# One layer, its first weight columns and its first norm: the order on ScalarE and the queues of the constant rows

## The chip, the core and the metric

The kernel runs on one core of a Trainium2 chip. The core has a matrix engine (TensorE, PE in the profile; its weight loads are PEld), a vector engine (VectorE, DVE), an engine for functions and scaled copies (ScalarE, ACT), a general one (GpSimd, POOL) and one that here only issues transfers (SyncE, SP). ACT and POOL issue transfers too. The metric is the device time of one execution in microseconds, the median of several runs.

## The reference

A hybrid decoder layer on one sequence of 2048 rows of 1024 numbers, in 32-bit floats:

```python
h = _rmsnorm(x, norm1_w[l])
proj = h @ w_in[l]
hg_p, rw_p = proj[..., :HG_COLS], proj[..., HG_COLS:]
...
o_hg = _hgrn2_mixer(q_raw, f_raw, i_raw, g_raw, lower_bounds[l], hg_norm_w[l])
rw_p = rw_p + (_token_shift(rw_p) - rw_p) * rw_shift_mu[l]
...
o_rw = _rwkv7_mixer(r, k, v, wd, ad, gd, ...)
x = x + jnp.concatenate([o_hg, o_rw], axis=-1) @ w_out[l]
x = x + _conv_ffn(_rmsnorm(x, norm2_w[l]), w_up[l], conv_w[l], conv_b[l], w_down[l])
```

with `_rmsnorm(x, w) = x * rsqrt(mean(x * x) + 1e-6) * w`. For the change only the first two lines matter: the norm of x and the product with `w_in` (1024 x 3840, thirty columns of 128).

## The kernel before

**Blocks and columns.** The sequence is worked in four blocks of 512 rows. For each block, `w_in` is taken in columns of 128: a job ("P") computes one column for 512 rows as eight steps over the inner dimension (`KD = 8`, index k). Every 32-bit operand is split into a high part and the rest (names ending in h and l), and a step is three matmuls, `wh*hh`, `wh*hl` and `wl*hh` (`mm3`), so a column is 24 matmuls into one bank (`pj`), which is then evicted by ScalarE and VectorE (`ev`). The first column is evicted by `ev_lora` (a scaled copy, two additions on VectorE, then a Tanh).

**The weights.** `load(i)` fetches column i as two halves (`wraw`, four buffers) by POOL's queue, and `split` makes `wh` with a cast on ScalarE (`S.copy`, line 249) and `wl` with a subtraction on VectorE (line 250). In the first block both parts are also stored to memory (`Win...`, four stores of 256 KB a column, POOL's queue), from where the later blocks read them. `wh` and `wl` have four buffers each, two columns' worth.

**The beginning.** Four tiles of 128 rows of x go by SP's queue into `first`. The small vectors (norm weights, biases and so on: eleven inputs, then `hg_lb_logits`) are loaded as rows of one 128 x 128 tile, `rows` (lines 143 to 149), alternately by POOL's and by ScalarE's queue; TensorE transposes it (`vps`), and VectorE copies it to `vt`, whose columns are the vectors. The norm of the first block (lines 151 and 152) is for each tile a square with a sum on ScalarE (`nsq`), a logarithm and an exponential (`nst`), and a scaling of x on VectorE. Then `transposed` turns the normed x on TensorE in eight groups of four transpositions (k = 0 to 7, six banks at hand, `hg` and `rw`), and `to_h` makes `hh` of each with a scaled copy on ScalarE and `hl` on VectorE (line 481). Job 0 calls for two of these groups first, then for one ahead of each of its eight steps.

**What sets the order.** The program states data flow; a scheduler orders the instructions of each engine by priority (earlier in the program first) and by its own model of when an instruction can start. Each engine then runs its list strictly in order, so an instruction that waits holds all behind it on that engine, issues of transfers among them. `tc.add_manual_dep(a, b, NOSYNC)` puts a behind b in that order without a wait of its own. ScalarE's functions need tables: `act` loads the table set when the function asks for another one, and puts the load behind all uses of the set before (`tab["uses"]`). Scaled copies (`AF.Copy`) and squares need none and are not in that list.

Of the kernel before, what the change touches and what calls it, by code (L numbers as in the profile page):

```python
# [11 lines left out]
AF = mybir.ActivationFunctionType  # L12
# [6 lines left out]
P = 128  # L19
# [45 lines left out]
def tile_layer(ctx, tc, consts, x, norm1_w, w_in, hg_lb_logits, hg_norm_w, rw_shift_mu, rw_w0, rw_w2,  # L65
# [20 lines left out]
    first = row_tile()  # L86
# [51 lines left out]
    with tc.tile_pool(name="vp", bufs=1, reuse_waits="tile") as vp, tc.tile_pool(name="ps0", bufs=1, space=PSUM, reuse_waits="tile") as pools["ps"]:  # L138
        rows = vp.tile([P, P], F32, name="rows")
        V.memset(rows, 0.0)  # L140
        n = 0
        queues = [nc.gpsimd.dma_start, S.dma_start]
        for nm, a, k in (("n1", norm1_w, 8), ("n2", norm2_w, 8), ("hgn", hg_norm_w, 4), ("mu", rw_shift_mu, 14),
                         ("w0", rw_w0, 4), ("a0", rw_a0, 4), ("kk", rw_k_k, 4), ("ka", rw_k_a, 4),
                         ("rk", rw_r_k, 4), ("lnw", rw_ln_w, 4), ("lnb", rw_ln_b, 4)):
            queues[len(off) % 2](rows[n:n + k, :], a.rearrange("o (k p) -> (o k) p", p=P))
            off[nm] = n
            n += k
        nc.gpsimd.dma_start(rows[n:n + 8, :], hg_lb_logits.rearrange("o (k p) -> (o k) p", p=P))
        off["lb"] = n  # L150
        for i in range(4):
            V.tensor_scalar_mul(first[:, i, :], first[:, i, :], rstd(vp, first[:, i, :], "nst", sqb=2))
        vps = pst("vps")
        TE.transpose(vps[:, :P], rows, ident)
        V.tensor_copy(vt, vps[:, :P])
# [89 lines left out]
    def split(pool, src, shape, name, bufs):  # L245

        hi = pool.tile(shape, F32R, tag=name + "h", name=name + "h", bufs=bufs)
        lo = pool.tile(shape, F32R, tag=name + "l", name=name + "l", bufs=bufs)
        S.copy(hi, src)  # L249
        V.tensor_sub(lo, src, hi.bitcast(F32))  # L250
        return hi, lo

# [16 lines left out]
    def phase1(c1):  # L269
# [207 lines left out]
            return f  # L477

        def to_h(k, tp, w):
            act(hh[:, k, :], tp, AF.Copy, scale=w)  # L480
            V.scalar_tensor_tensor(hl[:, k, :], tp, w, hh[:, k, :].bitcast(F32), ALU.mult, ALU.subtract)

        def to_h2(nb):
# [23 lines left out]
        def dense():  # L507

            rows[0] = first
            jobs = []  # L510
            for nb in range(NBLK):
                if nb >= 2:
                    jobs.append(("O", nb - 2))
                jobs.append(("A", nb))
                jobs.append(("P", 3584, ev_lora(nb), lambda nb=nb: done["rw1"] >= 2 * nb, None))
                for s_ in range(2):
                    if s_ == 1:
                        jobs.append(("P", 3712, ev_gd(nb), lambda nb=nb: done["rw2"] >= 2 * nb, None))
                    n_rw = 2 * nb + s_
                    for u in range(3):  # L520
                        for p in (2 * s_, 2 * s_ + 1):
                            jobs.append(("P", 2048 + u * 512 + p * P, ev_rkv(nb, p, u),
                                         lambda n=n_rw: done["rw1"] >= n,
                                         mark("rw") if (u == 2 and p == 2 * s_ + 1) else None))
                    for j in (2 * s_, 2 * s_ + 1):
                        n_hg = 4 * nb + j
                        for i, ev in enumerate((ev_q, ev_f, ev_v, ev_g)):
                            jobs.append(("P", i * 512 + j * P, ev(nb, j), lambda n=n_hg: done["hg"] >= n - 1,
                                         mark("hg") if i == 3 else None))
            jobs.append(("O", 2))  # L530


            at = [i for i, jb in enumerate(jobs) if jb[0] == "A"]
            extra = []
            for nb in range(NBLK):
                if nb + 1 < NBLK:
                    extra += [(at[nb] + 18, ("E", load4(nb + 1, x[0], (nb + 1) * BLK))),
                              (at[nb] + 22, ("E", norm4(nb + 1))), (at[nb] + 25, ("T", nb + 1))]
                if nb >= 2:
                    extra += [(at[nb] + 6, ("E", load4(("N", nb - 2), x1d[nb - 2], 0))),  # L540
                              (at[nb] + 10, ("E", norm4(("N", nb - 2)))), (at[nb] + 11, ("N", nb - 2))]
            for m in range(2):
                extra += [(at[3] + 14 + 5 * m, ("E", sum_load(m))), (at[3] + 17 + 5 * m, ("E", sum_make(m)))]
            extra += [(at[3] + 25 + m, ("W", 2, o_take(m))) for m in range(4)]
            for i, jb in sorted(extra, key=lambda e: e[0], reverse=True):
                jobs.insert(i, jb)
            cols = [jb[1] for jb in jobs if jb[0] == "P"]
            NCOL = len(cols) // NBLK
            Win = [[[dp.tile([P, 4, P], F32, name=f"Win{ct}{k2}{c}") for c in "hl"] for k2 in range(2)]
                   for ct in range(NCOL)]  # L550
            loaded = {}

            def load(i):
                if i < len(cols) and i not in loaded:
                    ws, ct = [], cols[i] // P
                    for k2 in range(2):
                        if i < NCOL:
                            raw = wp.tile([P, 4, P], F32, tag="wraw", name="wraw", bufs=4)
                            wload(raw, w_in[0, k2 * 512:k2 * 512 + 512, cols[i]:cols[i] + P].rearrange("(k p) c -> p k c", p=P))
                            ws.append(split(wp, raw, [P, 4, P], "w", 4))  # L560
                            for c in range(2):
                                nc.gpsimd.dma_start(Win[ct][k2][c], ws[k2][c].bitcast(F32))
                        else:
                            ws.append(tuple(wp.tile([P, 4, P], F32R, tag="w" + c, name="w" + c, bufs=4) for c in "hl"))
                            for c in range(2):
                                wload(ws[k2][c].bitcast(F32), Win[ct][k2][c])
                    loaded[i] = ws

            i = 0
            load(0)  # L570
            ahead = iter(())
            for n, jb in enumerate(jobs):
                if jb[0] == "E":
                    jb[1]()
                    continue
                if jb[0] == "A":
                    if jb[1] == 0:
                        banks = spread()
                        ahead = transposed(four_tiles(rows[0]), "n1", lambda: next(banks), to_h)
                    continue  # L580
                if jb[0] == "T":
                    yield from turn(jb[1])
                    continue
                if jb[0] == "N":
                    yield from transposed(four_tiles(rows.pop(jb)), "n2", lambda: bank("pj"), to_h2(jb[1]))
                    continue
                if jb[0] in "OW":
                    while done["rw2"] < 2 * jb[1] + 2 or done["hg"] < 4 * jb[1] + 4:
                        yield None
                    if jb[0] == "W":  # L590
                        jb[2]()
                    else:
                        yield from (out_block(2, *rows["O"]) if jb[1] == 2 else out_block(jb[1], then=jb[1] + 2))
                    continue
                _, col, ev, cond, fin = jb
                while not cond():
                    yield None
                load(i)
                ws = loaded.pop(i)
                if i == 0:  # L600
                    next(ahead)
                    next(ahead)
                    constants()
                load(i + 1)
                i += 1
                acc = bank("pj")
                then = jobs[n + 1][1] if jobs[n + 1][0] == "A" else None
                for k in range(KD):
                    wh, wl = ws[k // 4]
                    next(ahead, None)  # L610
                    mm3(acc, (wh[:, k % 4, :], wl[:, k % 4, :]), (hh[:, k, :], hl[:, k, :]), k == 0, k == KD - 1)
                    if k == KD - 1:
                        ev(acc)
                        if fin is not None:
                            fin()
                    next_block(then, k)
                    yield 648
# [957 lines left out]
```

## Time and profile before

| what | us |
| --- | --- |
| three runs | 2680.16, 2685.16, 2686.11 |
| median | 2685.16 |
| profiled execution | 2686.26 |
| its span, from the first to the last instruction | 2684.5 |

The profile is of one execution. Times in its views count from the start of the span. A row of a timeline has the start, the length, the engine, the line of the kernel, the operation, and the tiles as out<-in; a bracket at its end says how long the engine had been idle and what ended that. A letter q behind an engine's name means its queue, that is, the issue of a transfer and not the transfer itself. A row of the transfers has the size and the time from issue to landing. Several alike instructions in a row are merged (x2). The length of a matmul is modelled, the distance between two starts is not.

### The profile page before, as it was taken

What the parts mean: (1) busy time and instruction counts of PE and PEld (TensorE: products, weight loads), DVE (VectorE), ACT (ScalarE), POOL (GpSimd) and SP (SyncE); (2) the same over time, 40 slices, a digit from 0 to 9 for tenths busy, and PEclk for the clock granted to TensorE, in tenths of its full rate; (3) what the DMA queues carried; (4) which work ended last, traced back from release to release, by engine and by line L of the source; (5) the groups of instructions that cost most, each with busy time, mean ns of one, the idle gap of its engine ahead of it and who ended that gap; (6) DMA issues with size and microseconds to landing.
All of it is one profiled execution on the core that took longest, in us unless ns stands there. A gap on an engine that the chain in (4) does not pass through costs nothing.

```text
span 2684.5 us, 47831 instructions
## 1 busy us (share of the span) xinstructions
PE 2614.7 (97%) x18059; PEld 2091.1 (78%) x18059; DVE 1929.6 (72%) x3705; ACT 1338.3 (50%) x2158; POOL 381.8 (14%) x684
## 2 busy tenths in 40 slices
PE   7999999999999999999999999999999999999998
PEld 5777777777777777778778888887888888788887
DVE  4867757576466764657578789988998888676556
ACT  4555442454544545433357665456555545445444
POOL 6433222212222123222100000000000000000000
PEclk9999999999999999999899999999999999999999
DMA  8654543355643556834584458756764463898665
GB/s 304 198 166 162 166 135 117 115 161 195 197 149 116 157 161 214 290 115 132 160 272 149 134 184 267 243 171 194 259 200 149 149 202 124 311 325 282 203 192 184
DMA packets 312828, 510.52 MB, mean 190 GB/s; under 512 B 46879, under 2 KB 143509, under 8 KB 312597
## 3 DMA queue, kind: packets, MB, share of 16 engines
q1 hardware_dynamic: 258225, 329.65, 37.2%
q0 software_dynamic: 54304, 177.80, 20.3%
q8 instruction: 142, 2.33, 0.4%
q14 instruction: 89, 0.73, 0.1%
q10 hardware_dynamic: 68, 0.02, 0.0%
HBM read 373.13 MB, written 134.22 MB: 189 GB/s over the span
## 4 chain that ended last, share of the span: by engine, by line
PE 74%; DVE 7%; DMA 6%; issue 6%; ACT 5%; POOL 1%; SPq 0%; DVEq 0%; POOLq 0%; ACTq 0%
PE pj L265 8%; PE pj L266 7%; PE pj L267 7%; PE ua L265 5%; PE ua L267 5%; PE ua L266 5%; PE da L266 3%; PE da L267 3%; PE da L265 3%; PE ud L266 2%; PE ud L265 2%; PE ud L267 2%; PE hg L969 2%; PE db L265 2%; PE db L266 2%
## 5 line engine op out<-in xcount | busy, mean ns | idle before, releaser
L265 PE MATMUL pj<-hh,wh 128*128 128x512 f32 x960 | 404.1, 421 | 4.5 <-ACT rkv L120 1.7
L266 PE MATMUL pj<-hl,wh 128*128 128x512 f32 x960 | 377.9, 394 | 0.0
L267 PE MATMUL pj<-hh,wl 128*128 128x512 f32 x960 | 377.7, 394 | 0.0
L265 PE MATMUL ua<-Bh,uwh 128*128 128x512 f32 x704 | 275.9, 392 | 1.0 <-ACT m L120 0.9
L267 PE MATMUL ua<-Bh,uwl 128*128 128x512 f32 x704 | 274.3, 390 | 0.0
L266 PE MATMUL ua<-Bl,uwh 128*128 128x512 f32 x704 | 274.1, 389 | 0.0
L265 PEld LDWEIGHTS pj<-hh,wh 128*128 128x128 f32 x960 | 181.2, 189 | 59.6 <-issue 14.0
L267 PEld LDWEIGHTS pj<-hh,wl 128*128 128x128 f32 x960 | 181.0, 189 | 40.1 <-issue 0.6
L266 PEld LDWEIGHTS pj<-hl,wh 128*128 128x128 f32 x960 | 181.5, 189 | 38.7 <-issue 5.9
L249 ACT CAST uwh<-uraw 128x512 fp32r<-128x512 f32 x220 | 135.1, 618 | 138.0 <-PE ua L266 63.2
L250 DVE TENSOR_TENSOR dal<-draw,dah 128x512 fp32r<-128x512 f32 x138 | 95.3, 690 | 113.1 <-ACT dah L249 113.0
L250 DVE TENSOR_TENSOR uwl<-uraw,uwh 128x512 fp32r<-128x512 f32 x220 | 147.3, 686 | 34.8 <-ACT uwh L249 34.8
L249 ACT CAST dah<-draw 128x512 fp32r<-128x512 f32 x138 | 85.8, 622 | 167.3 <-PE da L266 78.7
L265 PEld LDWEIGHTS ua<-Bh,uwh 128*128 128x128 f32 x704 | 132.2, 188 | 29.8 <-ACT m L120 2.4
L267 PEld LDWEIGHTS ua<-Bh,uwl 128*128 128x128 f32 x704 | 132.2, 188 | 28.1 <-DVE uwl L250 0.4
L266 PEld LDWEIGHTS ua<-Bl,uwh 128*128 128x128 f32 x704 | 132.2, 188 | 26.6
L265 PE MATMUL ud<-Bh,uwh 128*128 128x512 f32 x352 | 138.0, 392 | 0.0
L267 PE MATMUL ud<-Bh,uwl 128*128 128x512 f32 x352 | 137.0, 389 | 0.0
L266 PE MATMUL ud<-Bl,uwh 128*128 128x512 f32 x352 | 137.0, 389 | 0.0
L1445 POOL DMA_DIRECT2D gd<-y x2 | 1.1, 556 | 947.0 <-DVE y L1443 947.0
L266 PE MATMUL da<-dbl,dah 128*128 128x512 f32 x332 | 129.5, 390 | 1.1 <-DVE dbl L250 1.1
L267 PE MATMUL da<-dbh,dal 128*128 128x512 f32 x332 | 129.2, 389 | 0.0
(570 smaller groups left out, 6199.2 us busy)
## 6 DMA issues: line engine op xcount, KB each, us to landing
uraw<-in_w_up_dram SPq DMA_DIRECT2D x176, 256.0 KB, 3.3
woraw<-in_w_out_dram POOLq DMA_DIRECT2D x96, 256.0 KB, 3.4
br<-gd SPq DMA_DIRECT2D x88, 256.0 KB, 4.1
draw<-Sg SPq DMA_DIRECT2D x88, 256.0 KB, 3.0
draw<-Tw SPq DMA_DIRECT2D x88, 256.0 KB, 3.5
gd<-y SPq DMA_DIRECT2D x86, 256.0 KB, 2.8
Sg<-br SPq DMA_DIRECT2D x72, 256.0 KB, 2.6
xt<-x1d SPq DMA_DIRECT2D x32, 512.0 KB, 5.9
```

The source lines that it names most:

```text
L249: S.copy(hi, src)
L250: V.tensor_sub(lo, src, hi.bitcast(F32))
L265: TE.matmul(acc, lh, rh, start=first, stop=False, skip_group_check=skip)
L266: TE.matmul(acc, lh, rl, start=False, stop=False, skip_group_check=skip)
L267: TE.matmul(acc, ll, rh, start=False, stop=last, skip_group_check=skip)
L969: TE.matmul(o, kt[:, t0:t0 + 64], qs, start=True, stop=True, tile_position=(0, e * 64))
L1445: (dma if end is None else nc.gpsimd.dma_start)(gd_[2 * h + b][fb * P:(fb + 1) * P, :], ys[0][:, b * BLK:(b + 1) * BLK])
```

## The change

Three things are changed in the beginning of the kernel.

- Of the eleven rows' transfers, POOL's queue issues the first, fifth and ninth, ScalarE's queue the other eight (before: six and five). The twelfth stays with POOL.
- `split` puts each of its casts behind the instructions in the list `behind`. During `load(0)` that list holds the last exponential of the norm. The call `load(1)`, which stood ahead of job 0's steps, moves into them, to k = 3, behind the call that makes `hh` of k = 5; during it the list holds that `hh`'s instruction. Then the list is emptied, and later calls of `split` are as before.
- `to_h` adds its scaled copy to the uses of the current table set, so that the load of the next set stands behind all eight.

```diff
-            queues[len(off) % 2](rows[n:n + k, :], a.rearrange("o (k p) -> (o k) p", p=P))
+            queues[len(off) % 4 > 0](rows[n:n + k, :], a.rearrange("o (k p) -> (o k) p", p=P))
...
             V.tensor_scalar_mul(first[:, i, :], first[:, i, :], rstd(vp, first[:, i, :], "nst", sqb=2))
+        behind = [tab["uses"][-1]]
...
-        S.copy(hi, src)
+        i_ = S.copy(hi, src)
+        for o_ in behind:
+            tc.add_manual_dep(i_.ins, o_.ins.name, NOSYNC, reason="rows first")
         V.tensor_sub(lo, src, hi.bitcast(F32))
...
         def to_h(k, tp, w):
-            act(hh[:, k, :], tp, AF.Copy, scale=w)
+            i_ = act(hh[:, k, :], tp, AF.Copy, scale=w)
+            tab["uses"].append(i_)
...
-                load(i + 1)
+                begin = i == 0
+                if not begin:
+                    load(i + 1)
                 i += 1
...
                 for k in range(KD):
                     wh, wl = ws[k // 4]
                     next(ahead, None)
+                    if begin and k == 3:
+                        behind[:] = tab["uses"][-1:]
+                        load(1)
+                        behind.clear()
```

## The prediction

> **What bounds the kernel now.** The page comes first: it says which engine fills the span, and where the few empty parts are.
>
> ```profile
> PE 2614.7 (97%) x18059; PEld 2091.1 (78%) x18059; DVE 1929.6 (72%) x3705; ACT 1338.3 (50%) x2158; POOL 381.8 (14%) x684
> PE   7999999999999999999999999999999999999998
> ```
>
> TensorE is busy for 97% of the span; only its first and last slice are not full. The change touches nothing but the first tens of microseconds, so next comes the same span cut at 12.30, 20.65, 24, 30.4 and 60 us (columns: span of the stretch, busy time of PE, PEld, DVE, ACT, POOL with instruction counts, clock, DMA share, GB/s).
>
> ```profile
> 0.00:12.30 12.30, 0.45 (x1) 0.18 (x1) 2.77 (x11) 5.63 (x12) 8.76 (x18) 1.00 0.85 300
> 12.30:20.65 8.35, 4.36 (x16) 2.87 (x16) 5.56 (x19) 5.60 (x13) 4.79 (x10) 1.00 0.98 303
> 20.65:24.00 3.35, 3.35 (x8) 2.50 (x9) 2.71 (x7) 1.69 (x3) 3.35 (x6) 1.00 0.59 220
> 24.00:30.40 6.40, 6.40 (x36) 5.11 (x35) 3.55 (x5) 3.34 (x6) 1.97 (x4) 1.00 0.54 126
> 30.40:60.00 29.60, 29.60 (x132) 24.54 (x131) 13.29 (x29) 12.24 (x21) 20.18 (x33) 1.00 0.99 357
> ```
>
> Before 20.65 us TensorE does one transposition of the constant rows and sixteen of x. From 20.65 on it has no gap until 60 us. So this stage is bound by the moment at which the first projection matmul can start, and every microsecond taken off that moment is worth a microsecond, as long as nothing behind it runs dry. The chain of waits, in order of time, says what sets the moment (start, length, what):
>
> ```profile
> 1.29 6.51 DMA wraw<-in_w_in_dram
> ...
> 10.76 7.20 DMA wraw<-in_w_in_dram
> 17.98 0.62 ACT wh L249
> 18.62 1.28 ACT L116
> 19.91 0.70 ACT hh L120
> 20.65 1.22 PE pj L265 x2
> ...
> 23.37 0.43 PE pj L266
> ...
> 24.18 0.24 PE pj L265
> ```
>
> Two loads of weights, a cast and a table load stand ahead of the first hh. The norm of x is not in it, though hh is made of normed x. ScalarE's own order of time shows why (start, length, engine, line, operation, out<-in; in brackets the idle time before and what ended it):
>
> ```profile
> 7.83 0.62 ACT L249 CAST wh<-wraw 128x512 fp32r<-128x512 f32 x1 [5.80 <-DMA wraw<-in_w_in_dram]
> 8.35 1.05 ACT L120 ACTIVATE nsq<-xt 128x1024 bf16<-128x1024 f32 x1
> ...
> 12.75 0.62 ACT L249 CAST wh<-wraw 128x512 fp32r<-128x512 f32 x1 [0.57 <-DMA wraw<-in_w_in_dram]
> 13.28 0.29 ACT L120 ACTIVATE nst<-nst,eps 128x1 f32<-128x1 f32 x1
> 13.47 1.04 ACT L120 ACTIVATE nsq<-xt 128x1024 bf16<-128x1024 f32 x1
> ...
> 14.71 0.28 ACT L120 ACTIVATE nst<-nst,eps 128x1 f32<-128x1 f32 x1
> 17.20 0.62 ACT L249 CAST wh<-wraw 128x512 fp32r<-128x512 f32 x1 [2.21 <-DMA wraw<-in_w_in_dram]
> 17.72 0.20 ACT L120 ACTIVATE nst<-nst 128x1 f32<-128x1 f32 x1
> ```
>
> ScalarE takes its instructions in order. The first cast holds it until 7.83, the second until 12.75, and the third, a cast for the second column of weights, until 17.20, with the last exponential of the norm (17.72) right behind. When x itself was there is read from its loads (issues with their starts; then the last one alone and the first one alone, with KB and us to landing):
>
> ```profile
> L88 SPq DMA_DIRECT2D xt<-in_x_dram x4: 328/374/425, 1.2 to 5.2; - x4
> xt<-in_x_dram SPq DMA_DIRECT2D x1, 512.0 KB, 5.0
> ```
> ```profile
> xt<-in_x_dram SPq DMA_DIRECT2D x1, 512.0 KB, 4.0
> ```
>
> The first quarter of x was issued at 1.2 and landed 4.0 later, at 5.2 (the second of these two rows). The last quarter of x was issued at 5.2 and landed 5.0 us later, at 10.2, yet its square began at 13.47.
>
> **The change, part by part.** *Norm ahead of casts.* The casts of column 0 get an order behind the last exponential of the norm, those of column 1 behind the hh of k=5. So the last square can begin at the landing, 10.2. From it on I use the durations of before:
>
> ```profile
> 17.95 0.75 DVE L152 TENSOR_SCALAR xt<-xt,nst 128x1024 f32<-128x1024 f32 x1 [2.15 <-ACT nst L120]
> ...
> 18.69 0.68 DVE L250 TENSOR_TENSOR wl<-wraw,wh 128x512 fp32r<-128x512 f32 x1
> 18.76 0.69 PE L259 MATMUL hg<-ident,xt 128*128 128x128 f32 x2 [2.10 <-DVE xt L152]
> ...
> 20.63 1.41 DVE L481 SCALAR_TENSOR_TENSOR hl<-hg,vt,hh 128x512 fp32r<-128x512 f32 x2
> ```
>
> Square to logarithm is 14.71 - 13.47 = 1.24, logarithm to exponential 0.28, exponential to the scaling of x 0.23 (17.72 to 17.95), scaling to transposition 0.81 (17.95 to 18.76), one transposition about 0.35 (half of 0.69). Sum from 10.2: 11.44, 11.72, 11.95, 12.76, 13.1. On ScalarE both casts of column 0 follow the exponential: 11.92 plus two steps of about 0.6 is 13.1 as well (0.6 is a cast's length). So hh of k=0 begins near 13.2 and the first matmul, 0.74 after it (19.91 to 20.65), near 13.9: 6.7 us earlier. The second matmul product needs hl. VectorE now does the scaling (to 12.7), two wl at 0.68 and then hl, which starts at about 14.1 to 14.2, against 20.63 before: 6.4 us earlier. I take the smaller, **6.4 us**.
>
> Bounds of that: if the order of ScalarE puts the last two squares ahead of the third tile's logarithm, VectorE scales two tiles in a row behind them, 0.75 later (5.7). If the last load of x lands 0.7 us later, since weights now share the queues with it, 5.7 too; both, 5.0. If it lands up to 0.6 earlier, 7.0.
>
> *Table load behind the split.* The 1.28 us at 18.62 leave the chain; the load now stands behind the hh of k=7. Without it alone hh would have begun at about 18.76 + 0.35, not at 19.91: 0.8 us, already inside the 6.4. What covers it now: the next function that needs its table is the Tanh of the first column's result at 32.55, some 4 us behind the last hh at 28.23. Without that cover it would cost 1.28.
>
> ```profile
> 25.80 0.69 ACT L120 ACTIVATE hh<-rw,vt 128x512 fp32r<-128x512 f32 x1 [0.21 <-PE rw L259]
> ...
> 28.23 0.69 ACT L120 ACTIVATE hh<-hg,vt 128x512 fp32r<-128x512 f32 x1 [0.52 <-PE hg L259]
> 30.32 0.62 ACT L249 CAST wh<-wraw 128x512 fp32r<-128x512 f32 x1 [1.41 <-PE pj L266]
> ...
> 32.55 0.63 ACT L120 ACTIVATE tl<-tl 64x512 f32<-64x512 f32 x1 [1.02 <-DVE tl L308]
> ```
>
> *Column 1 behind hh of k=5.* That hh ended at 26.49, so at 20.1 after a shift of 6.4. Two casts and two wl follow, to about 22.0. Column 0 ended at 30.3 (where the release of its weights let the cast at 30.32 go), so column 1 starts at 23.9: about 2 us to spare. If the casts fall behind the last hh (28.92, now 22.5), the first wl is done at 23.9: still nothing, at the edge.
>
> *Constant rows.* POOL issues four of them instead of seven, ScalarE eight instead of five.
>
> ```profile
> 5.18 0.50 POOL L149 DMA_DIRECT2D rows<-in_hg_lb_logits_dram  x1
> 8.09 0.78 POOL L559 DMA_DIRECT2D wraw<-in_w_in_dram  x1 [2.41 <-DMA wraw<-in_w_in_dram]
> ...
> 22.58 1.51 POOL L559 DMA_DIRECT2D wraw<-in_w_in_dram  x2
> ```
>
> POOL's second weight load, its ninth transfer (the one of 1.29, seven rows, then this), waited until the first had landed. I read that as a limit of eight transfers in flight; with three rows fewer it goes out near 4.2. It landed at about 12.7 before (the cast at 12.75), and it is needed at 12.5 now, so this part is worth between 0 and 0.3. ScalarE's three more issues cost at most 3 x 0.6 = 1.8 us in its 5.8 idle us ahead of 7.83, and its first square cannot start before the first x is there (5.2). If the last of the eight waits for the second x to land, the first three squares have still some 3 us, as many as they need, until 10.2. Zero.
>
> The Trainium skill, DMA: Bandwidth & Descriptors, Rules for kernel authors, speaks against a gain here: spreading transfers over issuing engines gives no bandwidth, it only saves issue time. By that rule the second weight load lands no earlier than 12.7, and the sum is 6.3 instead of 6.4.
>
> *Does the gain last?* Behind the start the weight loads must keep up. They have room:
>
> ```profile
> 41.55 0.62 ACT L249 CAST wh<-wraw 128x512 fp32r<-128x512 f32 x1 [2.88 <-DMA wraw<-in_w_in_dram]
> ...
> 46.73 0.68 ACT L120 ACTIVATE rkv<-pj,omu 128x512 f32<-128x512 f32 x1
> ```
>
> DMA is 99% busy from 30.4 to 60, and two casts waited for it. The later of column 4's casts, at 41.55, is ready with its wl at 42.9, and TensorE wants it half a column (12 x 0.227 = 2.7) behind the end of column 3, whose result is read at 46.73: at 49.4: 6.5 us to spare. Even if this load did not move at all, the shift just uses it up. And it will move, since DMA was only 54 to 59% busy between 20.65 and 30.4. So nothing is given back: 0, at worst about 1.
>
> **Sum.** The profiled execution took 2686.26 (span 2684.5, so 1.8 outside it); less 6.4 is 2679.9. The median of the runs, 2685.16, lies 1.1 lower: 2678.8. I say **2679.0**, 6.2 us or 0.23% under the median; its own range, by the bounds 5.0 to 7.0 and a microsecond of spread to either side, is 2677 to 2681.5.
>
> **The rivals.**
> *Slow clock.* The chain shows matmuls 0.43 apart until 24.2 and 0.24 behind, while the clock column of the stretches says 1.00 throughout, so the pace is read from the spacing. If the fast pace comes at a time of its own and not with the work, TensorE works from 14.2 to 24.2 at half pace and loses 5.0 us there, where before it lost half of 3.5, 1.75. The gain shrinks by 3.2 to 3.0, time 2682. For it: no row tells what released the pace. Against it: it came 3.5 us after matmuls became dense, and the transpositions ahead of it did not bring it. In the Trainium skill, TensorE: Matmul & The Clock Gate, The HAM clock gate, the window that releases the clock is free-running and takes one busy window of about 3.4 us. By that the earlier start costs 0 to 1.7 us in a given execution.
>
> *Part of the gain only*: ScalarE's order comes out with a cast still waiting for a load, or the issues of rows wait and the squares with them. One such wait is worth 2.2 (that of 17.20): 2681.2.
>
> *Slower: POOL runs one column behind.* POOL issues the stores of split weights and the next loads in one order. Before, loads ran two columns ahead (22.58 for column 3, while column 0 was computed). If the loads of column 2 now stand behind the stores of column 1, which wait for casts moved behind hh, they go out near 23, land 7.2 later (as the load of 10.76 did), and with cast and subtraction are ready near 31.6: 2 us late for column 2's start at 29.3 (23.9 plus 24 matmuls at 0.227). The next column's loads wait for those stores in turn, go out near 34, land near 41 and are ready at 43, 8 late for 34.7. It decides from that second column on: 2679 + 8 = 2687, and more with each column. Against it: column 2's buffers come free with column 0's split near 14, and nothing moves its loads by name.
>
> *Not what it says*: the casts waited for loads that x delays as well, and only the table load's 0.8 goes: 2684.4. The landing at 10.2 speaks against it.
>
> **Chances.** Forecast 0.62, slow clock 0.11, part only 0.10, POOL 0.13, nothing moved 0.04. Two executions of this kernel can be told apart at about 0.2%, 5.4 us, so the forecast lies just beyond that bound: of its 0.62, some 0.53 fall under 2679.8 and the rest within; slow clock, part and nothing add to within, POOL and a stray 0.02 to slower. Faster 0.54, same 0.31, slower 0.15. The range takes in the part-gains and the case of nothing moved: 2674 to 2686; beyond it POOL's case is left out.
>
> **What would show it.** Right: first square near 5.3, last one near 10.3, both casts of column 0 behind the last exponential, the first projection matmul at 13.5 to 15, the table load behind the eighth hh, no gap on TensorE from there to 60. Wrong: a first matmul behind 16; a cast ahead of an exponential with DMA as its releaser; 0.43 spacing for more than 7 us; POOL's loads of column 2 behind the stores of column 1 and TensorE waiting for wh or wl between 24 and 60.

## The result, and the profile after

The change made the kernel slower. Nine runs each:

| | before | after |
| --- | --- | --- |
| median, us | 2682.04 | 2695.18 |
| lowest to highest | 2679.68 to 2691.91 | 2683.30 to 2698.41 |
| profiled execution | 2686.26 | 2695.18 |
| its span | 2684.5 | 2693.3 |

The ratio of after to before is 1.0034, 95% interval [1.0022, 1.0046]. That is some 9 us, less than the 13 between the two medians and near the ratio of the two means (1.0032): the times of one kernel spread over 12 to 15 us, so single medians are rough.

Stretches of after's span, cut where the prediction cut, and one more behind (columns as there):

```profile
12.30:20.65 8.35, 7.13 (x23) 5.18 (x24) 7.44 (x20) 5.26 (x13) 5.12 (x11) 1.00 0.62 206
30.40:60.00 29.60, 27.33 (x111) 21.29 (x110) 10.00 (x21) 9.52 (x16) 16.53 (x28) 0.94 0.90 298
60.00:430.00 370.00, 362.15 (x3465) 282.63 (x3464) 260.12 (x647) 182.18 (x288) 121.02 (x207) 1.00 0.52 168
```

TensorE is busier than before up to 20.65 (7.13 against 4.36). Between 30.4 and 60 it does 111 matmuls where it did 132, at a clock of 0.94, and is empty for 2.27 us where it had no gap. So there was a gain, and then a larger loss. What TensorE waited for in the first 100 us (sum, times, longest), in after and then in before:

```profile
PE rw L724 <- DVE KB L712: 3.6, 1, 3.6
...
PE pj L268 <- ACT wh L250: 1.5, 1, 1.5
PE pj L268 <- DVE lastc L312: 0.7, 1, 0.7
```
```profile
PE rw L714 <- DVE KB L702: 0.5, 1, 0.5
```

Three waits are new or longer: one for the read-out of a column (lastc), one for a cast (wh), one for KB, behind the column products. They stand in TensorE's order of time at these places:

```profile
17.48 0.80 PE L268 MATMUL pj<-hh,wh 128*128 128x512 f32 x1
...
38.85 0.47 PE L268 MATMUL pj<-hh,wh 128*128 128x512 f32 x1 [0.74 <-DVE lastc L312]
...
43.38 0.50 PE L268 MATMUL pj<-hh,wh 128*128 128x512 f32 x1 [1.54 <-ACT wh L250]
...
45.55 0.63 PE L269 MATMUL pj<-hl,wh 128*128 128x512 f32 x1
45.98 0.63 PE L270 MATMUL pj<-hh,wl 128*128 128x512 f32 x1
...
89.03 1.67 PE L724 MATMUL rw<-AR,KB 64*128 64x128 f32 x16 [3.61 <-DVE KB L712]
```

The first projection matmul starts at 17.48 against 20.65: 3.2 us gained. Behind the two waits the matmuls stand 0.43 apart for a while (45.55 to 45.98) instead of 0.23; the clock of the stretch from 45.0 to 48.5 is 0.52. Eight matmuls 0.2 slower are 1.6 us, and the two waits with the stretched matmuls around them some 3, which makes 4.9 between 36 and 60 us (the lag below goes from -2.8 to +2.1).

To compare whole runs I match the matmuls of two traces one by one, in the order of each tile name, and take how much later each starts than in before: its lag, in us, median of the matmuls in a stretch.

```
stretch        20-24  30-36  42-50  50-60  70-82  90-100  150-300  2300-2680
after           -3.2   -2.8   +1.3   +2.1   +2.1    +6.7     +5.8       +8.5
```

The head start of 3 us turns into a lag of 2.1 at 50 us and of 6.7 at 90 us, and the rest is already there. Behind 100 us the lag of any kernel wanders by a few us in an execution, so below I read it up to 100. A part of the early lag is chance too: behind the same first projection matmul, near 17.5, the first record of the full clock stands at 16.88 in the run e2 below and at 21.25 in after, and their lags at 30 to 36 us differ by 1.4.

**Why the start gained 3.2 and not 6.4.** SP's loads of x (issues with first and last start), then ScalarE's order of time:

```profile
L88 SPq DMA_DIRECT2D xt<-in_x_dram x4: 328/374/423, 1.2 to 7.2; - x4
```
```profile
2.79 0.43 ACTq L146 DMA_DIRECT2D rows<-in_rw_k_k_dram  x1
5.15 0.25 ACTq L146 DMA_DIRECT2D rows<-in_rw_k_a_dram  x1
...
5.79 0.31 ACTq L146 DMA_DIRECT2D rows<-in_rw_ln_b_dram  x1
...
12.92 1.06 ACT L120 ACTIVATE nsq<-xt 128x1024 bf16<-128x1024 f32 x1 [2.71 <-DMA xt<-in_x_dram]
...
16.74 1.27 ACT L120 ACTIVATE hh<-hg,vt 128x512 fp32r<-128x512 f32 x2 [0.99 <-PE hg L262]
...
25.89 1.28 ACT L116 ACT_TABLE_LOAD   x1
...
36.39 0.62 ACT L250 CAST wh<-wraw 128x512 fp32r<-128x512 f32 x1 [5.74 <-DMA wraw<-in_w_in_dram]
36.91 0.69 ACT L120 ACTIVATE rkv<-pj,omu 128x512 f32<-128x512 f32 x1
42.70 0.62 ACT L250 CAST wh<-wraw 128x512 fp32r<-128x512 f32 x1 [5.11 <-DMA wraw<-in_w_in_dram]
...
67.90 0.62 ACT L250 CAST wh<-wraw 128x512 fp32r<-128x512 f32 x1 [3.06 <-DMA wraw<-in_w_in_dram]
68.43 0.68 ACT L120 ACTIVATE rkv<-pj,omu 128x512 f32<-128x512 f32 x1
```

ScalarE's queue issues five rows, stands still from 3.2 to 5.15 and then issues the other three. SP's last load of x is issued at 7.2 instead of 5.2, and its square starts at 12.92, when it has landed, instead of near 10.2. The trace shows the link: the issues of both queues take eight completion semaphores (numbers 108 to 115) in turn, and an issue waits until the transfer that had its semaphore before has landed. In before the last load of x comes to the semaphore of x's first quarter (landed 5.19, issue 5.21), in after, with three more rows in between, to that of the second quarter (landed 7.20, issue 7.21).

**Where the time went.** The same list shows it. A cast of column 3 waits 5.74 us for its load, and the eviction of column 1 (rkv, at 36.91) stands behind it in ScalarE's order. The products have two banks, so column 3's first one, at 38.85, needs the bank of column 1: this is the wait for lastc. The cast for the second half of column 3 waits 5.11, and at 43.38 TensorE waits for it: the wait for wh. POOL's order of time says why these loads are late, in after and then in before:

```profile
19.87 1.52 POOL L563 DMA_DIRECT2D wraw<-in_w_in_dram  x2
24.37 0.56 POOL L566 DMA_DIRECT2D Win160h<-wh  x1 [2.98 <-ACT wh L250]
...
26.53 0.76 POOL L563 DMA_DIRECT2D wraw<-in_w_in_dram  x1
28.10 0.54 POOL L566 DMA_DIRECT2D Win170h<-wh  x1 [0.81 <-ACT wh L250]
...
37.30 0.54 POOL L566 DMA_DIRECT2D Win200h<-wh  x1 [6.87 <-ACT wh L250]
38.03 0.54 POOL L566 DMA_DIRECT2D Win200l<-wl  x1 [0.18 <-issue]
38.56 2.99 POOL L563 DMA_DIRECT2D wraw<-in_w_in_dram  x4
```
```profile
28.00 0.56 POOL L562 DMA_DIRECT2D Win170h<-wh  x1 [3.90 <-ACT wh L249]
...
29.42 0.76 POOL L559 DMA_DIRECT2D wraw<-in_w_in_dram  x1
```

In before both loads of column 3 (22.58 x2, shown in the prediction) go out ahead of the stores of column 2 (Win17), and then one load between each two stores. In after only the first load of column 3 does (26.53). The second, with both of column 4 and one of column 5, stands behind the stores of column 2 and of the first half of column 3 (Win200), and that store waits 6.87 us for the cast of 36.39, which waits for the load of 26.53. So the second load of column 3 goes out at 38.56, 15 us later than before (22.58 plus one issue of 0.75). No line of the change names these loads: the scheduler wrote POOL's list anew.

### The profile page after: what moved, and what is told of

Its sections match the earlier page's. It is cut to its first block, busy times and chain, and to the rows that moved or that the text cites. A ratio compares the mean times of both kernels' runs of the same rounds, so it can differ in the third digit from the quotient of the medians.

```text
span 2693.3 us, 47829 instructions
## 1 busy us (share of the span) xinstructions
PE 2618.8 (97%) x18059; PEld 2091.5 (78%) x18059; DVE 1927.1 (72%) x3705; ACT 1337.2 (50%) x2158; POOL 379.2 (14%) x681
## 4 chain that ended last, share of the span: by engine, by line
PE 76%; DVE 7%; DMA 7%; ACT 5%; issue 3%; POOL 1%; SPq 1%; DVEq 0%; ACTq 0%; POOLq 0%
PE pj L268 8%; PE pj L269 7%; PE pj L270 7%; PE ua L268 5%; PE ua L269 5%; PE ua L270 5%; PE da L269 3%; PE da L270 3%; PE da L268 3%; PE ud L269 3%; PE ud L270 3%; PE ud L268 3%; PE hg L979 2%; PE db L270 2%; PE db L269 2%
```

## The experiments

I held two theories. A: the loads stand too late in POOL's order; ScalarE's casts wait for them, in order, with evictions behind them, and TensorE waits for both. B: x's last quarter, late by 2.7 us, is what costs. Medians of 7 to 12 runs of each kernel and 31 to 35 of before on the same chip (before: 2685.03, 2685.26 and 2686.33 for the first four, the next four and the last four); lags as above.

| run | median, us | ratio to before, 95% | lag 30-36 | 50-60 | 90-100 |
| --- | --- | --- | --- | --- | --- |
| e1_rows_undone | 2693.85 | 1.0026 [1.0015, 1.0037] | -3.2 | +2.3 | +6.1 |
| e2_loads_ahead | 2685.62 | 1.0002 [0.9990, 1.0013] | -4.2 | -2.3 | -2.3 |
| e3_loads_ahead_rows_undone | 2688.49 | 1.0017 [1.0004, 1.0029] | -2.7 | +0.2 | +0.2 |
| e4_rows_alone | 2691.52 | 1.0020 [1.0008, 1.0032] | -4.1 | -2.1 | +6.2 |
| e5_before_loads_ahead | 2686.07 | 0.9995 [0.9986, 1.0005] | -1.4 | -1.4 | -1.4 |
| e6_lb_behind_norm | 2683.41 | 0.9994 [0.9981, 1.0007] | -5.6 | -2.3 | -2.3 |
| e7_only_casts_of_column_1 | 2683.12 | 0.9997 [0.9988, 1.0007] | -2.9 | -2.9 | -2.9 |
| e8_column_1_and_loads_ahead | 2687.15 | 1.0002 [0.9991, 1.0013] | -2.9 | -2.9 | -2.9 |
| e9_evictions_first | 2685.12 | 0.9998 [0.9987, 1.0009] | -4.5 | -4.5 | -3.9 |
| e10_all_mended | 2682.97 | 0.9988 [0.9980, 0.9997] | -6.3 | -5.3 | -4.7 |
| e11_table_load_alone | 2682.02 | 0.9988 [0.9977, 0.9999] | -2.1 | -2.1 | -2.1 |
| e12_norm_and_table_alone | 2694.35 | 1.0025 [1.0012, 1.0037] | -3.5 | -1.3 | +5.6 |

e1, e4 and e12 are like after: slower than before beyond their intervals, and at +5.6 to +6.2 by 100 us. Of the kernels with a negative lag there none is slower beyond its interval. e3, at +0.2, lies between; it is slower beyond its interval as well.

**The rows' queues undone, in after.**

```diff
-            queues[len(off) % 4 > 0](rows[n:n + k, :], a.rearrange("o (k p) -> (o k) p", p=P))
+            queues[len(off) % 2](rows[n:n + k, :], a.rearrange("o (k p) -> (o k) p", p=P))
```

> The changed kernel with the constant rows alternating between POOL's and ScalarE's queue again, as before the change. POOL's order of transfers is then: loads of columns 0 and 1 early, loads of column 2 behind column 0's stores, and the loads of columns 3 and 4 behind all eight stores of columns 1 and 2. Theory A (loads that POOL issues too late stall ScalarE's casts, and with them TensorE): the last quarter of x is issued at 5.2 instead of 7.2 and the first projection matmul is at 14 to 14.7 instead of 17.5, but column 3 still waits: TensorE idle for more than 2 us between 25 and 60, and the time is not below the kernel before (2681 to 2695). Theory B (the late last quarter of x is what costs): the time falls to 2674 to 2679, without gaps between 25 and 60. Theory C (only a different interleaving behind 100 us costs): lag at 80 us below the kernel before, loss behind that.

x's last load goes out at 5.1 again (after: 7.2). Yet the first projection matmul stands at 17.36 and the lag at 100 us is +6.1. Theory B falls: the landing is mended, the loss stays. ScalarE's order of time shows what took the place of the late landing:

```profile
13.03 0.21 ACT L120 ACTIVATE ltmp<-ltmp 128x8 f32<-128x8 f32 x1 [2.76 <-DVE ltmp L168]
...
13.57 1.04 ACT L120 ACTIVATE nsq<-xt 128x1024 bf16<-128x1024 f32 x1
...
39.59 0.62 ACT L250 CAST wh<-wraw 128x512 fp32r<-128x512 f32 x1 [6.53 <-DMA wraw<-in_w_in_dram]
```

The exponential of the lower bound (ltmp) needs the constant rows, and the scheduler put it ahead of the third tile's logarithm and of the last square; that square starts at 13.57, although x was there some 3 us earlier. And the loads of columns 3 and 4 stand in POOL's list behind all eight stores of columns 1 and 2, so a cast waits 6.53.

**The loads ahead of the stores, written by hand, in after**, and the same with the rows undone:

```diff
+            def fetch(i):
+                if i < NCOL and i not in raws:
...
+                    fetch(i)
+                    fetch(i + 1)
...
-                            raw = wp.tile([P, 4, P], F32, tag="wraw", name="wraw", bufs=4)
-                            wload(raw, w_in[0, k2 * 512:k2 * 512 + 512, cols[i]:cols[i] + P].rearrange("(k p) c -> p k c", p=P))
+                            raw = raws[i][k2]
```

> The changed kernel with one edit: the loads of column i+1 are written ahead of the split and stores of column i in the first block, so that POOL's order has the pair of loads of column 3 ahead of column 2's stores and so on. x is as late as in the changed kernel. Theory A: first projection matmul at 17.5 as in the changed kernel, no gap on TensorE from 25 to 60, rkv evictions no more than 1 us behind their column's end, the bubble of 3.6 at 89 gone or under 1; time 2677 to 2681, about 3 under the kernel before. Theory B: nothing changes, 2690 to 2697. Theory C: the early gaps go and the time still stays over 2686.

> Both edits: rows alternate again, and loads of column i+1 stand ahead of column i's stores. Theory A: first projection matmul at 14 to 14.7, no gap to 60, time 2674 to 2679, 3 to 7 under the kernel before. Theory B: the same first matmul, and 2674 to 2679 too, but then the run with rows alone undone gives that as well. Theory C: over 2684.

This one edit takes the lag at 100 us from +6.7 to -2.3 and the median from 2695 to 2685.6, with the late quarter of x still in it. That is theory A's main test. The 2677 to 2681 that was expected did not come: against before, a lag of -2.3 does not show in the median. What is left of TensorE's waits between 24 and 100 us in e2:

```profile
PE pj L268 <- DVE lastc L312: 1.6, 1, 1.6
PE rw L734 <- DVE KB L722: 0.5, 1, 0.5
```

The long wait for KB is gone with the late casts. In e3 the first projection matmul, expected at 14 to 14.7, is at 17.15, behind the lower bound's exponential as in e1; the same wait for lastc is 2.6 us, and the lag ends at +0.2; its ratio stays above 1, which that lag does not explain.

**The rows' queues alone, and the loads ahead alone, in before.**

```diff
-            queues[len(off) % 2](rows[n:n + k, :], a.rearrange("o (k p) -> (o k) p", p=P))
+            queues[len(off) % 4 > 0](rows[n:n + k, :], a.rearrange("o (k p) -> (o k) p", p=P))
```

> The kernel before with the queues of the constant rows changed alone. ScalarE's order in it already has all four squares ahead of the casts, since the eight issues fill its time until x lands; POOL's order has the loads of columns 2 and 3 behind the eight stores of columns 0 and 1, and those of 4 and 5 behind the eight stores of 2 and 3. Theory A: last quarter of x issued near 7.2, first projection matmul near 17 to 18, gaps on TensorE between 25 and 60 of 1 to 5 us, time 2683 to 2694. Theory B: slower or equal by the late x alone: the first matmul is still earlier than 20.65, so the time is 2679 to 2682. If the moved load of column 1 alone spoils POOL's order, this kernel shows no gap.

> The kernel before with the loads of column i+1 written ahead of column i's stores, and nothing else: the control for the run in which the changed kernel got that edit. Theory A (in the changed kernel late loads stall ScalarE's casts and evictions, and the edit removes just that): the kernel before has no TensorE gap for the edit to remove, so its time stays at 2682 to 2687 and the first matmul at 20.6. Rival D (the edit is worth some 10 us on any order of the beginning, as it lightens the transfers): 2673 to 2678.

The rows' part, which I had priced at nothing, costs 0.2% by itself. It moves no weight load in the program, but POOL's list comes out with four loads behind the eight stores of two columns, and the casts wait:

```profile
28.12 0.62 ACT L249 CAST wh<-wraw 128x512 fp32r<-128x512 f32 x1 [4.64 <-DMA wraw<-in_w_in_dram]
...
42.48 0.62 ACT L249 CAST wh<-wraw 128x512 fp32r<-128x512 f32 x1 [4.18 <-DMA wraw<-in_w_in_dram]
```

The loads written ahead are no gain that the times show: e5 is at 0.9995 of before, although column 1's loads go out ahead of column 0's stores. The first projection matmul, expected at 20.6, is at 18.30, and a lag of -1.4 is kept from 30 us on. So in e2 the edit paid because it undid a harm.

**The lower bound's exponential behind the norm**, in e3's kernel:

```diff
-    act(ltmp[:, 4:12], ltmp[:, 4:12], AF.Exp)
+    lb_ = act(ltmp[:, 4:12], ltmp[:, 4:12], AF.Exp)
+    tc.add_manual_dep(lb_.ins, behind[0].ins.name, NOSYNC, reason="rows first")
```

> The changed kernel with rows alternating again, loads ahead, and one order more: the exponential of the lower bounds (ltmp), which needs all constant rows, stands behind the last exponential of the norm. With rows alternating it stood in front of the third tile's logarithm and held ScalarE until 13.0. Theory A': with that wait gone the last square begins at the landing of x near 10.2 and the first projection matmul is at 14.3 to 15.3, 2 to 3 earlier than in any variant so far; of this the columns up to 5 give back what their loads are late, so the gap near column 3 grows by about as much: lag at 60 us between -4 and 0, time 2679 to 2686. If late loads do not bind: lag at 60 us near -6 and time 2676 to 2679.

The first projection matmul comes at 16.09, later than the 14.3 to 15.3 expected, and the lag reaches -5.6. Then 3.3 us are given back in one place (TensorE's order of time, then ScalarE's):

```profile
38.39 0.47 PE L269 MATMUL pj<-hh,wh 128*128 128x512 f32 x1 [3.02 <-DVE lastc L313]
```
```profile
34.28 0.62 ACT L251 CAST wh<-wraw 128x512 fp32r<-128x512 f32 x1 [6.38 <-DMA wraw<-in_w_in_dram]
35.93 0.62 ACT L251 CAST wh<-wraw 128x512 fp32r<-128x512 f32 x1 [1.02 <-DMA wraw<-in_w_in_dram]
```

These are casts of column 3; the eviction of column 1, whose bank TensorE waits for, stands behind them.

**Column 1's casts behind the second hh and the table load, without the norm and the rows**; then with the loads ahead as well. This is near the change's part on column 1 but not the same: `load(1)` keeps its old place, and its casts stand behind `hh` of k = 1, not of k = 5. `split` and `to_h` are as in the change, and `behind` begins empty.

```diff
+                behind[:] = tab["uses"][-1:] if i == 0 else []
                 load(i + 1)
+                behind.clear()
```

> The kernel before with two orders only: the table load behind the eight hh, as in the changed kernel, and the casts of column 1 behind the second hh, with the load of column 1 left at its old place; rows and the casts of column 0 as before. POOL's order stays close to that of before (both loads of column 3 ahead of column 2's stores, one load between stores from then on). Theory A: last exponential of the norm near 15.0 instead of 17.7, first projection matmul near 17, no gap of more than 1 us on TensorE to 60; lag at 60 and at 100 us -2.5 to -3.6; time 2680 to 2683. Rival C (any shift of the start is lost in the stages behind): lag at 60 us negative, lag at 1000 us zero or above.

> The same two orders with the loads written ahead as well. Theory A: as the run without, first projection matmul near 17, lag at 60 us -2.5 to -3.6, time 2680 to 2683, since no load was late there.

The first projection matmul is at 17.60: without the norm's and the rows' parts the start is as early as in after. And nothing is lost: POOL's loads stay between the stores, TensorE's only wait between 24 and 100 us is 0.5 us for KB, as in before, and the -2.9 of the start is kept to 100 us. e8 is alike (17.51, and the same lag). In the median it does not show (0.9997): 3 us of 2685 are at the edge of what these runs tell.

**Evictions ahead of casts, in after.** `shift_mix` records its scaled copy, and the casts of column i + 1 stand behind that of column i - 1, which frees the bank that column i + 1 needs:

```diff
-            act(y, acc, AF.Copy, scale=omu[:, i:i + 1])
+            tab["ev"] = act(y, acc, AF.Copy, scale=omu[:, i:i + 1])
...
+                    behind[:] = [tab["ev"]] if i < 10 else []
                     load(i + 1)
...
+                    behind.clear()
```

> The changed kernel, and one thing more: from column 2 to column 10 the casts are ordered behind the scaled copy by which ScalarE reads the column before out (the last eviction), so a cast that waits for a late load no longer stands ahead of an eviction in ScalarE's order; the loads' place isn't written by hand. Theory A (loads issued late on POOL reach TensorE through ScalarE's in-order casts): first projection matmul still at about 17.5 (lag -3.2); POOL's order now takes the loads in pairs, one column ahead of the stores that need casts, so the pair of column 3 is issued near 25 to 28 and not 38; TensorE's gap of 0.7 that DVE's lastc ends is gone; lag at 60 us between -3 and 0 and at 100 us below +1, time 2681 to 2687, about 9 us under the changed kernel. If only the place of the loads matters and not the order of casts and evictions, a gap of 1 to 3 us with ACT's wh as releaser stands in its place. Theory B (x's last quarter late is what costs): first matmul and all behind it as in the changed kernel, lag +5 or more at 100 us, 2693 or more.

No load is moved by hand, and the late quarter of x is still there (its square starts at 12.66). TensorE's waits between 24 and 100 us are now:

```profile
PE rw L726 <- DVE KB L714: 1.1, 1, 1.1
```

The median is 2685.12, 10 us under after (0.9998 of before instead of 1.0034). With the casts held, the scheduler wrote POOL's list in pairs, two loads ahead of each column's four stores. So this run mends both halves of theory A at once, the loads' place and the block on ScalarE, and does not tell which was worth more; e2 mended the loads' place alone and kept 1.6 us of the block.

**All mended:** after with the rows undone, the exponential behind the norm, the loads ahead and the evictions first.

> The changed kernel with four edits: rows on the two queues as before the change, the exponential of the lower bound behind the norm's last one, loads of column i+1 written ahead of column i's stores, and evictions ahead of the next casts as in the run before. Theory A: first projection matmul near 16.1 as where the exponential was put behind the norm (lag -4.8), and the 3.0 us gap near 37 (DVE's lastc, a cast waiting for its load ahead of the eviction) gone, so lag -4.5 to -6 is kept to 100 us; time 2679 to 2682, ratio 0.998 to 0.999: this would be faster than both kernels. Rival: the DMA queues are the limit (99% busy between 30 and 60 before), so the loads land as late as before whatever the order, and the wait only changes its name to ACT's wh: lag at 60 us -2 to -3, time 2683 to 2685, no different from before.

The start is the best of all, 15.39, and between 24 and 100 us TensorE waits 0.7 for lastc and 1.2 for KB. The lag stays at -4.7 up to 100 us. The median is 2682.97 against 2686.33: 0.9988, with an interval that just leaves out 1. The rival, that the DMA queues make the loads late whatever the order, holds in small part: a cast of column 3 still waits 3.83 for its load. But column 1's eviction on ScalarE stands ahead of it, at 29.27 (in e6 at 36.45, behind the casts). The 0.7 us that are left have the same cause on VectorE: the subtraction that waits for the late cast stands ahead of the last step of column 1's read-out (lastc).

```profile
34.45 0.69 DVE L254 TENSOR_TENSOR wl<-wraw,wh 128x512 fp32r<-128x512 f32 x1 [3.58 <-ACT wh L251]
35.06 0.15 DVE L313 COPY lastc<-pj 128x1 f32<-128x1 f32 x1
```

**The table load's part alone, in before.**

```diff
-            act(hh[:, k, :], tp, AF.Copy, scale=w)
+            i_ = act(hh[:, k, :], tp, AF.Copy, scale=w)
+            tab["uses"].append(i_)
```

> The kernel before, with only the table load's part: the eight hh are put on the list that holds the next load of a table back. POOL's order is that of before. If the load's 1.28 us was worth what the prediction reckoned, hh of k=0 begins 0.7 to 0.8 earlier (19.1 to 19.2, behind its transposition) and the first projection matmul near 19.9; the load stands behind the eighth hh, hidden; lag -0.7 to -0.8 kept to 100 us, time within 1 us of before's. If the load then holds the Tanh of column 0 or its eviction, the lag goes to +0.5 by 60 us.

The load stands at 26.78, behind the eighth hh, and hides. hh of k=0 starts at 17.74, 2.2 earlier, more than the 0.8 worked out:

```profile
16.92 0.62 ACT L249 CAST wh<-wraw 128x512 fp32r<-128x512 f32 x1 [0.53 <-DMA wraw<-in_w_in_dram]
17.74 1.27 ACT L120 ACTIVATE hh<-hg,vt 128x512 fp32r<-128x512 f32 x2 [0.20 <-PE hg L259]
```

The cast ahead of it was at 17.98 in before: 1.1 of the 2.2 came from a load that landed earlier in this execution. The other 1.1 I put to the table load. e11's ratio equals e10's, though its lag at 100 us is -2.1 against -4.7, and its median is 4.3 us under before's where 1 was expected: the medians do not separate gains of this size.

**Norm ahead of casts and the table load, without the rows and column 1.**

```diff
-                begin = i == 0
-                if not begin:
-                    load(i + 1)
+                load(i + 1)
+                behind.clear()
...
-                    if begin and k == 3:
-                        behind[:] = tab["uses"][-1:]
-                        load(1)
-                        behind.clear()
```

> The changed kernel without the rows' queues and without holding the casts of column 1 behind the sixth hh: only the casts of column 0 behind the norm, and the table load. POOL's order comes out with four loads (columns 2 and 3) behind all eight stores of columns 0 and 1, four more behind those of columns 2 and 3. Theory A: first projection matmul near 17.3 (the lower bound's exponential again ahead of the third tile's logarithm), loads of columns 2 and 3 issued near 22 to 24, casts that wait 4 us or more for a load between 28 and 45, TensorE gaps of 2 us or more by 60 us, lag at 100 us between +2 and +7, time 2689 to 2695. If holding column 1's casts was what spoiled POOL's order, the loads keep up here: no gap above 0.5 us, lag -3 kept, 2682.

Here `load(1)` is called while the list still holds the norm's last exponential, so the casts of both columns stand behind it (14.66 to 17.36), not only those of column 0. Four loads stand behind eight stores, as in e4, and TensorE's waits are like those of after, with ScalarE's mk in the place of lastc (24 to 100 us):

```profile
PE rw L719 <- DVE KB L707: 3.9, 1, 3.9
PE pj L268 <- ACT wh L250: 1.7, 1, 1.7
PE pj L268 <- ACT mk L120: 1.7, 1, 1.7
```

So each of two parts is enough to spoil POOL's list, the norm ahead of the casts (e12; in e1 with column 1's part) and the rows' queues (e4). The table load alone is not (e11), nor is it together with the casts of column 1 behind the second hh (e7); the move of `load(1)` to k = 3 was not run alone. One thing the four spoiled kernels have in common: column 0's first cast stands behind the norm's last exponential, at 14.6 to 15.2, in e4 by the scheduler's own choice; in before, e7 and e11 it is at 7.4 to 7.8. A late cast makes the first stores late, and the loads come out behind them. That this is what turned the list is not shown: no run looks into the scheduler's model.

## Why the prediction was wrong

- **"So the last square can begin at the landing, 10.2"** was right as a mechanism, but not what this change brings about. In e10 it begins at 10.27, and the last exponential stands at 11.76 (worked out: 11.72). In after x was not there; and in e1, where it was, the exponential of the lower bound, which the prediction does not have, held the square until 13.57.
- **"Constant rows. ... Zero"** is the step that failed in the start. I had seen a limit of eight transfers in flight on POOL's queue and applied it to ScalarE's eight rows, but not to SP beside them. With eight rows on ScalarE, SP issues x's last load at 7.2 (after, e4); with five rows it is at 5.1 to 5.2 (before, e1). SP and ScalarE take one set of eight semaphores in turn, POOL another. It cost 2.7 us of landing. The bound written for a late landing was 0.7. The part failed once more in POOL's list, which it spoils by itself (e4). The second weight load did go out at 4.17 in after, as worked out, and landed 5.7 later, near 9.9 and not at 12.7; nothing waited for it.
- **"exponential to the scaling of x 0.23 ..., scaling to transposition 0.81 ..., one transposition about 0.35"** were sized too small. e10, with x in time, has its first projection matmul at 15.39 and not at 13.9. TensorE's order of time in e10:

```profile
10.75 0.45 PE L155 MATMUL vps<-ident,rows 128*128 128x128 f32 x1 [10.75 <-DMA rows<-in_hg_lb_logits_dram]
11.58 0.69 PE L263 MATMUL hg<-ident,xt 128*128 128x128 f32 x2 [0.38 <-DVE vt L156]
...
14.62 0.64 PE L263 MATMUL rw<-ident,xt 128*128 128x128 f32 x2
15.39 0.80 PE L269 MATMUL pj<-hh,wh 128*128 128x512 f32 x1
```

  All sixteen transpositions of x stand behind that of the constant rows, which land at 10.75. They take from 11.58 to near 15, back to back, and the one that the first hh needs is the thirteenth, at 14.19 (worked out: 12.76). I had priced the last one and taken the others as done. VectorE was nearly as late: it copies the constant rows (vt, at 11.23) ahead of scaling three of the four tiles, and scales the last one at 13.12, that is 1.36 and not 0.23 behind the exponential. The start of e10 is 5.3 us earlier than before's, not 6.4.
- **"Does the gain last? ... So nothing is given back: 0, at worst about 1"** is the step that turned the sign. The 6.5 us to spare were reckoned with POOL's order of before. In after, the lag goes from -2.8 to +6.7: 9.5 us given back, 4.9 of it by 60 us (two waits and the slow clock behind them) and 4.6 at 82 to 90 (one wait of 3.61, and a slow clock again). The second part has the same cause: the loads stay late, and a cast that waits 3.06 us for its load, at 67.90, holds an eviction to 68.43, against 63.05 in before. KB is worked out behind it, and TensorE waits 3.61 for KB. In the nine experiments other than e1, e4 and e12 the wait for KB is 0.5 to 1.2.
- **The rival "POOL runs one column behind"** had the right queue and the right mechanism, stores that wait for casts ahead of loads, at 8 us and a chance of 0.13. The place was wrong: column 2's loads went out at 19.87, in time, and it was columns 3 to 5. The argument against it, "nothing moves its loads by name", was the mistake: the order on a queue is the scheduler's, and it may change for instructions that no line of the diff touches.
- **The table load and column 1** went as worked out: the load at 25.89, hidden (e11 too), and no wait for column 1's casts: in after TensorE has its first wait behind 17.48 at 38.
- **"Slow clock"** as put, that the pace would come at a time of its own, fell: the matmuls stand 0.23 apart from 16.5 on in e10 and from 24.2 on in before. It cost after little: 3.8 us at half pace (17.48 to 21.25) where before had 3.4 (20.65 to 24.02). The argument that transpositions do not bring the pace fell too: in e2 the first record of the full clock, at 16.88, is ahead of the first projection matmul, at 17.52, and behind transpositions alone. *Part of the gain only* came true for the start and was overtaken by the loss; *Not what it says* fell with the 3.2 us that the start did gain.

## What to carry to other kernels

Where a scheduler orders a queue, an order constraint on one engine can rewrite the list of another: before pricing an edit, ask which loads share a queue with stores that wait for the engine that is being reordered, and write the loads ahead by hand if they matter. Where one engine both casts what arrives and reads out what is done, put the read-out first, since a cast that waits for a load blocks it. Where two queues take their semaphores from one set, as SP and ScalarE do here, small transfers moved onto one can delay a large one on the other.

## What the runs showed of the hardware

- Eight small transfers on ScalarE's queue instead of five held back SP's fourth load of x by 2 us (7.2 against 5.2), though their rows are 2 to 7 KB each. The wait is for one of eight semaphores that the two share; whether a queue has a limit of its own, no run here shows.
- After a wait of 2.8 to 4.0 us for KB near 88 us, TensorE ran at half pace for a window of 3.4 us in after, e1 and e12 and of 6.8 in e4; after one of 0.5 to 1.2, in before and the nine other kernels, it did not. Such a window also followed e1's wait of 3.38 at 41, and in after two waits of only 0.74 and 1.54 us, 4.5 us apart. But one of 3.02, near 38, in e6 brought none, nor did one of 2.62, near 41, in e3, nor 1.72 and 1.70 in e12. The Trainium skill, TensorE: Matmul & The Clock Gate, HAM oscillation, has gaps of over about 3.4 us as those to avoid. By that the waits of 4.0 (e4), 3.9 (e12) and 3.61 (after) should count and the others not; the windows behind 0.74 and 1.54, and in e1 behind 2.8, do not agree with it.
- What fits better is where a wait falls. In each execution the granted clock changes at times that are whole numbers of 3.41 us apart (45.15 and 89.52 in after, 41.10 and 88.89 in e1). Counted within windows of that grid up to 100 us, 2.3 to 3.3 us of idle time in one window was followed by half pace each time (after, e1 twice, e4, e12), and up to 1.8 was not: the 3.02 us of e6 are 1.67 in one window and 1.35 in the next. One window with 1.54 in after, ahead of 45.15, is against it, and e4's second one, with 1.26, stayed at half pace; so the rule is an inference from these traces and not shown.
